# MLP ramp of a hybrid encoder: residual and first-phase tiles in one pool, casts of late right factors ordered behind PSUM copies

## The chip, the cores and the metric

One core of one Trainium2 chip. The metric is the device time of one execution in microseconds (us), as the median of several runs. All times below are of the kernel before.

## The reference

Two layers on a sequence of 1024 tokens with 1024 features, float32: layer 0 mixes tokens with grouped-query attention, layer 1 with a bidirectional gated linear attention. Behind each mixer stands a dense MLP with a squared ReLU and 4096 hidden features; a final RMSNorm ends it. The change touches only the two MLPs:

```
def sq_relu_mlp(h, w_in, w_out):
    return jnp.square(jax.nn.relu(h @ w_in)) @ w_out
...
        h = h + sq_relu_mlp(rmsnorm(h, norm_mlp[i]), mlp_w_in[i], mlp_w_out[i])
```

## The kernel before

Activations lie transposed: features on the 128 partitions, 512 tokens (one half) along the free dimension. Each float32 product is made of three matmuls on rounded parts: a value is split into a high part (a cast on ScalarE, L97) and a low part (a subtraction on VectorE, L98), and high by high, high by low and low by high are added in PSUM (`mm_into`, L463).

`layer_rest` (L755) runs twice, once per layer: the mixer's output projection with the residual, then the MLP's first phase (`h @ w_in`, `mlp_in`), then its second (`mlp_out`). Both phases use a scheme of seven products for two-by-two blocks in place of eight. P1 to P7 each multiply a combination of weight blocks (the left factor: `Weights.combine`, L483, four VectorE steps L487 to L490, then a split) with a combination of blocks of the normalised residual (the right factor). The right factors of the first phase are made once per layer:

- B11, B21: the normalised first half (features 0 to 511 and 512 to 1023); T1 and T2: differences, made at L831 and L841. These serve P1, P2, P5 and P6.
- T3: four subtractions at L846, then four splits; it serves P7.
- B22: four splits of the normalised second half, for P3.
- T4: four subtractions at L853, then four splits, for P4.

The first phase walks over eight groups of four hidden tiles each; a group's seven products have 24 matmuls each, twelve per output tile. P1, P6, P7 and P4 accumulate in two "a" banks of PSUM (there are four), P2 in two "b" banks, P5 and P3 in two "b" banks again (there are only two of these, so the P5 of the next group needs the P3 of this one drained). Results leave PSUM in `run` (L540): P1, P5 and P6 by a copy on ScalarE (L558) into a tile s1, s5 or s2; P2, P7 and P3 by an addition on VectorE (L561), followed by ReLU and square on ScalarE (L506, L507); P3 also by three subtractions (L570 to L575); P4 by L506, L507 and L582. The finished tiles are stored to DRAM by SyncE (L534).

The order of the first two groups (the ramp) is P1 and P2 of group 0, P1 and P2 of group 1, then P5, P6, P7, P3 of group 0, P5 and P6 of group 1, P4 of group 0, P7, P3 and P4 of group 1. The left factor of a step is prepared two steps ahead (`prep`), the weights' blocks are loaded by SyncE (L481) as soon as one of six buffers is free.

The framework that the kernel is written in orders the instructions of each engine when the program is built: by priority, which is the order of the source unless `tc.high_priority(offset=...)` shifts it, among what its plan takes to be ready. The queues are then worked off in that order. In the kernel before, T3, B22 and T4 carry negative offsets of 40, 80 and 160, so that they stand later than where they are written.

The sixteen residual tiles lie in a pool `hp`, next to scratch tiles (`tmpr`). The first phase's result tiles other than s1 of the first two groups come from a pool `hid` of sixteen that is opened behind T4, once `hp` and the scratch are closed, on the same memory:

```
859                     mid.close()
860                     hid_pool.append(pool_of(one, "hid", 16, side="right"))
861                     for g, p in ramp:
...
867                         run(g, p)
```

Of the kernel before, what the change touches and what calls it, by code (L numbers as in the profile page):

```python
# [23 lines left out]
F32 = mybir.dt.float32  # L24
F32R = mybir.dt.float32r
AF = mybir.ActivationFunctionType
# [5 lines left out]
P = 128  # L32
# [3 lines left out]
HN = S // 2  # L36
# [5 lines left out]
NCH = S // P  # L42
LEAD = 22
LAG = 3
LATER = 40


C_MIX0, C_MLP0, C_MIX1, C_MLP1, C_FIN, C_QA, C_QB, C_KA, C_KB, C_OUT, NCOL = 0, 8, 16, 24, 32, 40, 41, 42, 43, 44, 46
# [2 lines left out]
def trunk_kernel(tc, xT, wqk, wv, wo, win0, wout0, gqk, gv, gvz, gr, gate, gwo, win1, wout1, cols, rope, cmat, yT):  # L51
    nc = tc.nc

    def pool_of(stack, name, bufs=1, side=None):
        return stack.enter_context(tc.tile_pool(name=name, bufs=bufs, side=side, reuse_waits="tile"))

    with ExitStack() as top:
# [135 lines left out]
        with ExitStack() as at:  # L193
            env.raw, env.tmp = wraw, pool_of(at, "tmp")
            right = at.enter_context(ExitStack())
# [18 lines left out]
            x = (xh, xl)  # L214
# [224 lines left out]
            for step in range(256):  # L439
                h = step // 16  # L440
# [63 lines left out]

        def relu_sq(t, src):
            nc.scalar.activation(out=t, in_=src, func=AF.Relu)  # L506
            nc.scalar.activation(out=t, in_=t, func=AF.Square)  # L507

        B11, B21, B22, T1, T2, T3, T4 = range(7)
        RIGHT = {"P1": B11, "P2": B21, "P3": B22, "P4": T4, "P5": T1, "P6": T2, "P7": T3}  # L510
# [1 line left out]
        def mlp_in(win, x, hx, hid, hid_dram):  # L512

            blocks = win.rearrange("(j i a) p (b n) -> j a b p i n", i=2, a=2, b=2)
            ngr = NPAIR // 2
            weights, factors, alpha, beta, tiles = {}, {}, {}, {}, {}

            def begin(g):
                if g < ngr:
                    weights[g] = Weights(lambda r, c: blocks[g, r, c], env.raw, ("11", "12") if g == 1 else ("22", "11", "21", "12"))  # L520

            def prep(g, p):
                factors[g, p] = weights[g].factor(p)

            def combine():
                weights[0].combine(False)
                begin(1)

            def reload():
                weights[0].load("22")  # L530
                weights[1].load("22", "21")

            def store(g, i, what, t):
                nc.sync.dma_start(out=hid_dram[what, 2 * g + i], in_=t)  # L534

            def tile_of(g, nm):
                pl = hx if g < 2 and nm == "s1" else hid
                return pl.tile([P, HN], F32, tag="hx", name=nm)

            def run(g, p):  # L540
                wh, wl = factors.pop((g, p))
                xs = x[RIGHT[p]]
                if p == "P1":
                    alpha[g] = [bank("a") for _ in range(2)]
                if p in ("P2", "P5"):
                    beta[g] = [bank("b") for _ in range(2)]
                for i in range(2):
                    ps = (alpha if p in ("P1", "P6", "P7", "P4") else beta)[g][i]
                    parts = []
                    for k in range(4):  # L550
                        ks = slice(i * HN + k * P, i * HN + k * P + P)
                        parts.append((wh[:, ks], wl[:, ks], xs[0][k], xs[1][k]))
                    mm_into(ps, parts, p in ("P1", "P2", "P5"))
                    t = tiles.setdefault((g, i), {})
                    if p in ("P1", "P6", "P5"):
                        nm = {"P1": "s1", "P6": "s2", "P5": "s5"}[p]
                        t[nm] = tile_of(g, nm)
                        nc.scalar.copy(out=t[nm], in_=ps)  # L558
                    elif p in ("P2", "P7", "P3"):
                        c = t[{"P2": "s1", "P7": "s5", "P3": "s2"}[p]]  # L560
                        nc.vector.tensor_tensor(out=c, in0=ps, in1=c, op=ALU.add)  # L561
                        relu_sq(c, c)
                        if p == "P2":
                            store(g, i, B11, c)
                        elif p == "P7":
                            store(g, i, B22, c)
                        else:
                            h11, h22 = t["s1"], t["s5"]
                            t1 = tile_of(g, "t1")
                            nc.vector.tensor_tensor(out=t1, in0=c, in1=h11, op=ALU.subtract)  # L570
                            store(g, i, T1, t1)
                            t["t2"] = t2 = tile_of(g, "t2")
                            nc.vector.tensor_tensor(out=t2, in0=h22, in1=t1, op=ALU.subtract)
                            store(g, i, T2, t2)
                            nc.vector.tensor_tensor(out=c, in0=h22, in1=c, op=ALU.subtract)  # L575
                            store(g, i, T3, c)
                    else:
                        c = tile_of(g, "h21")
                        relu_sq(c, ps)
                        store(g, i, B21, c)  # L580
                        t4 = tile_of(g, "t4")
                        nc.vector.tensor_tensor(out=t4, in0=c, in1=t["t2"], op=ALU.subtract)  # L582
                        store(g, i, T4, t4)

            rest = ("P5", "P6", "P7", "P3", "P4")
            steps = [(g, p) for g in (0, 1) for p in ("P1", "P2")] + [(g, p) for g in (0, 1) for p in rest]
            steps = steps[:8] + [(1, "P5"), (1, "P6"), (0, "P4")] + steps[11:]
            steps += [(g, p) for g in range(2, ngr) for p in ("P1", "P2") + rest]
            return steps, begin, prep, run, combine, reload
# [165 lines left out]
        def layer_rest(w, src, o, gcol, win, wout, last, ahead, begun):  # L755


            hid_dram = dram.tile([7, NPAIR, P, HN], F32, name=f"hid_dram{last}")
            hm_dram = dram.tile([KT, P, S], F32, name=f"hm_dram{last}")
            with ExitStack() as ph:  # L760
                env.raw = Turns((wraw, 2), (pool_of(ph, "mraw", 4), 4))
                with ExitStack() as one:
                    hx = pool_of(one, "hx", 4, side="right")
                    mid = one.enter_context(ExitStack())
                    hp = pool_of(mid, "hp", side="right")
                    scratch = mid.enter_context(ExitStack())
                    env.tmp = pool_of(scratch, "tmpr", side="right")
                    big2 = pool_of(one, "big2", 8)
                    ht = halves(KT)
                    at_slot = [(0, 0)] + [(4 + k, 1) for k in range(3, -1, -1)] + [(k, 1) for k in range(3, -1, -1)]  # L770
                    at_slot += [(4 + k, 0) for k in range(3, -1, -1)] + [(k, 0) for k in range(3, 0, -1)]
                    for m, half in at_slot:
                        ht[m][half] = hp.tile([P, HN], F32, name=f"h{m}_{half}")
                    x = [([None] * 4, [None] * 4) for _ in range(7)]
                    r = [None, None]

# [11 lines left out]
                        return t  # L788

                    todo = []  # L790
                    hid_pool = []
                    steps, begin, prep, run, combine, reload = mlp_in(win, x, hx, SimpleNamespace(tile=lambda *a, **k: hid_pool[0].tile(*a, **k)), hid_dram)
                    weights_ahead = iter(steps)
                    for half in range(2):
                        sums = SumSquares(nc.vector if half else nc.gpsimd)
                        for m in range(KT):
# [9 lines left out]
                            ps = begun.pop(0) if begun else proj("b" if m % 4 == 0 else "a", wm, o, half)  # L806
                            h = ht[m][half]
# [3 lines left out]
                            for _ in range(2):  # L811
                                if todo:
                                    k = todo.pop(0)
# [27 lines left out]
                        nc.vector.tensor_tensor(out=t2, in0=normed(4 + k, 1), in1=ht[k][0], op=ALU.subtract)  # L841
                        xsplit(T2, k, t2, big)
                    prep(*next(weights_ahead))
                    with tc.high_priority(offset=-LATER):
                        for k in range(4):
                            nc.vector.tensor_tensor(out=ht[k][1], in0=ht[4 + k][1], in1=ht[k][1], op=ALU.subtract)  # L846
                            xsplit(T3, k, ht[k][1], big)
                    with tc.high_priority(offset=-2 * LATER):
                        for k in range(4):
                            xsplit(B22, k, ht[4 + k][1], big)  # L850
                    with tc.high_priority(offset=-4 * LATER):
                        for k in range(4):
                            nc.vector.tensor_tensor(out=ht[4 + k][0], in0=ht[4 + k][0], in1=t2s[k], op=ALU.subtract)  # L853
                    scratch.close()
                    big3 = pool_of(one, "big3", 4)
                    with tc.high_priority(offset=-4 * LATER):
                        for k in range(4):
                            xsplit(T4, k, ht[4 + k][0], big3)
                    mid.close()
                    hid_pool.append(pool_of(one, "hid", 16, side="right"))  # L860
                    for g, p in ramp:
                        nxt = next(weights_ahead, None)
                        if nxt:
                            prep(*nxt)
                        if p == "P5":
                            begin(g + 1) if g else None
                        run(g, p)
                env.tmp = pool_of(ph, "tmp2", side="right")
                raw2 = pool_of(ph, "raw2", 4)
                hst = pool_of(ph, "hst", 3)  # L870
# [2 lines left out]
                ht = halves(KT)  # L873
# [397 lines left out]
```

## Time and profile before

| what | value |
|---|---|
| median of 3 runs | 2391.19 us (2389.13 to 2392.6) |
| the profiled execution, its own time | 2392.76 us |
| its span, first to last instruction | 2390.8 us |
| mean granted TensorE clock, share of full speed | 0.987 |
| busy share of TensorE / VectorE / ScalarE / GpSimd | 96% / 75% / 56% / 14% |
| the two MLP ramps in the span | about 648 to 734 us and 1740 to 1826 us |

In the profile's rows PE is TensorE's matmuls, PEld its weight loads, DVE VectorE, ACT ScalarE, POOL GpSimd and SPq the queue of SyncE, which issues DMAs. L12 is line 12 of the kernel. In a timeline each row has the start and the duration in us, the engine, the line, the operation, the tile written and the tiles read, the shapes and the count; a number in square brackets is the time that the engine stood idle before it, with what it waited for. Consecutive instructions of one engine overlap at their ends, so the pitch from start to start is shorter than the duration.

### The profile page before, as it was taken

What the parts mean: (1) busy time and instruction counts of PE and PEld (TensorE: products, weight loads), DVE (VectorE), ACT (ScalarE), POOL (GpSimd) and SP (SyncE); (2) the same over time, 40 slices, a digit from 0 to 9 for tenths busy, and PEclk for the clock granted to TensorE, in tenths of its full rate; (3) what the DMA queues carried; (4) which work ended last, traced back from release to release, by engine and by line L of the source; (5) the groups of instructions that cost most, each with busy time, mean ns of one, the idle gap of its engine ahead of it and who ended that gap; (6) DMA issues with size and microseconds to landing.
All of it is one profiled execution on the core that took longest, in us unless ns stands there. A gap on an engine that the chain in (4) does not pass through costs nothing. (4 is left out here: it accounts for less than half of the span.)

```text
span 2390.8 us, 29877 instructions
## 1 busy us (share of the span) xinstructions
PE 2302.1 (96%) x10710; PEld 1899.9 (79%) x10710; DVE 1781.9 (75%) x2502; ACT 1346.5 (56%) x2386; POOL 335.8 (14%) x267
## 2 busy tenths in 40 slices
PE   8889999999979999999999999999979999999996
PEld 6677777777868888888888888898868888888885
DVE  8989999995786565888776767667686656797785
ACT  7448888884455555543344755655455555543343
POOL 2434444443000000000012000000100000000003
PEclk9989999999989999999999999999989999999998
DMA  5442111104435546954522121115625445965422
GB/s 177 129 141 62 43 38 45 36 14 147 144 119 168 175 161 222 309 187 151 175 91 85 47 73 53 54 71 189 216 71 192 160 165 176 320 211 185 150 89 71
DMA packets 157796, 317.50 MB, mean 133 GB/s; under 512 B 15048, under 2 KB 17872, under 8 KB 157520
## 3 DMA queue, kind: packets, MB, share of 16 engines
q1 hardware_dynamic: 157648, 315.60, 39.6%
q8 instruction: 84, 1.38, 0.2%
q14 instruction: 64, 0.52, 0.1%
HBM read 223.20 MB, written 92.27 MB: 132 GB/s over the span
## 5 line engine op out<-in xcount | busy, mean ns | idle before, releaser
L98 DVE TENSOR_TENSOR wl<-raw,wh 128x1024 fp32r<-128x1024 f32 x293 | 360.5, 1230 | 199.9 <-ACT wh L97 198.0
L97 ACT CAST wh<-raw 128x1024 fp32r<-128x1024 f32 x293 | 307.4, 1049 | 325.5 <-PE ps_a L467 134.3
L97 ACT CAST hh<-hst 128x512 fp32r<-128x512 f32 x224 | 134.8, 617 | 247.2 <-PE ps_a L468 112.5
L148 POOL TENSOR_TENSOR sq<-sq 128x512 f32<-128x512 f32 x35 | 54.5, 1557 | 1399.4 <-ACT sq L146 785.2
L401 POOL TENSOR_TENSOR pl<-p,ph 128x512 fp32r<-128x512 f32 x128 | 181.8, 1421 | 198.7 <-ACT p L398 129.7
L467 PE MATMUL ps_a<-xl,wh 128*128 128x512 f32 x512 | 201.2, 393 | 0.0
L466 PE MATMUL ps_a<-xh,wh 128*128 128x512 f32 x512 | 200.8, 392 | 0.0
L466 PE MATMUL ps_a<-hh,wh 128*128 128x512 f32 x512 | 199.4, 389 | 1.4 <-ACT h L506 1.4
L468 PE MATMUL ps_a<-xh,wl 128*128 128x512 f32 x512 | 200.1, 391 | 0.0
L98 DVE TENSOR_TENSOR hl<-hst,hh 128x512 fp32r<-128x512 f32 x224 | 153.1, 702 | 63.1 <-ACT hh L97 62.3
L467 PE MATMUL ps_a<-hl,wh 128*128 128x512 f32 x512 | 199.3, 389 | 0.6 <-DVE hl L98 0.6
L468 PE MATMUL ps_a<-hh,wl 128*128 128x512 f32 x512 | 199.2, 389 | 0.0
L278 DVE TENSOR_REDUCE mx<-ps_b 128x1 f32<-128x512 f32 x256 | 169.5, 683 | 12.6 <-PE ps_b L277 10.2
L466 PE MATMUL ps_b<-xh,wh 128*128 128x512 f32 x384 | 150.2, 391 | 26.9 <-ACT s L558 26.9
L397 ACT ACTIVATE ph<-ps_a 128x512 fp32r<-128x512 f32 x248 | 148.2, 598 | 29.7 <-PE ps_a L391 27.4
L398 ACT ACTIVATE p<-ps_a 128x512 f32<-128x512 f32 x256 | 152.2, 596 | 1.0 <-POOL pl L401 0.2
L467 PE MATMUL ps_b<-xl,wh 128*128 128x512 f32 x384 | 149.9, 390 | 0.0
L468 PE MATMUL ps_b<-xh,wl 128*128 128x512 f32 x384 | 149.4, 389 | 0.0
L506 ACT ACTIVATE s<-s 128x512 f32<-128x512 f32 x96 | 60.7, 632 | 111.1 <-DVE s L561 111.1
L277 PE MATMUL ps_b<-k,q 128*128 128x512 f32 x256 | 105.8, 415 | 9.4 <-DVE mx L278 9.4
L466 PEld LDWEIGHTS ps_a<-xh,wh 128*128 128x128 f32 x512 | 96.9, 189 | 21.2 <-ACT s L558 0.9
L466 PEld LDWEIGHTS ps_a<-hh,wh 128*128 128x128 f32 x512 | 96.1, 188 | 22.1 <-ACT h L506 2.3
(277 smaller groups left out, 5986.3 us busy)
## 6 DMA issues: line engine op xcount, KB each, us to landing
raw<-in_win_dram SPq DMA_DIRECT2D x80, 512.0 KB, 3.7
raw<-in_wout_dram SPq DMA_DIRECT2D x80, 512.0 KB, 3.6
hst<-hid_dramFalse SPq DMA_DIRECT2D x56, 512.0 KB, 3.8
hst<-hid_dramTrue SPq DMA_DIRECT2D x56, 512.0 KB, 3.5
q<-q_dram SPq DMA_DIRECT2D x96, 128.0 KB, 2.8
hid_dramFalse<-s SPq DMA_DIRECT2D x48, 256.0 KB, 2.8
hid_dramFalse<-t SPq DMA_DIRECT2D x48, 256.0 KB, 3.2
hid_dramTrue<-s SPq DMA_DIRECT2D x48, 256.0 KB, 2.0
```

Source lines behind the costliest of these rows:

```text
L97: nc.scalar.copy(out=hi, in_=src)
L98: (leng or nc.vector).tensor_tensor(out=lo, in0=src, in1=hi.bitcast(F32), op=ALU.subtract)
L148: self.eng.tensor_tensor(out=sq, in0=self.acc, in1=sq, op=ALU.add)
L277: nc.tensor.matmul(ps, q1[h][:, c * P : c * P + P], kst[h // 4][0][:, HALF[half]], start=True, stop=True)
L278: nc.vector.tensor_reduce(out=mx[h][:, half * 8 + c : half * 8 + c + 1], in_=ps, axis=AX.X, op=ALU.max, negate=True)
L397: nc.scalar.activation(out=phh, in_=ps, func=AF.Exp)
L398: nc.scalar.activation(out=p, in_=ps, func=AF.Exp)
L401: (nc.vector if c % 2 == 0 else nc.gpsimd).tensor_tensor(out=pll, in0=p, in1=phh.bitcast(F32), op=ALU.subtract)
L466: nc.tensor.matmul(ps, wh, xh, start=start and i == 0, stop=False, skip_group_check=not start)
L467: nc.tensor.matmul(ps, wh, xl, start=False, stop=False, skip_group_check=not start)
L468: nc.tensor.matmul(ps, wl, xh, start=False, stop=i == len(parts) - 1, skip_group_check=not start)
L506: nc.scalar.activation(out=t, in_=src, func=AF.Relu)
```

## The change

The pool `hid` is opened before the residual is made, and the sixteen residual tiles are taken from it with the tag of the result tiles, in the order rows 0 to 3 and 4 to 7 of the two halves as shown. A result tile therefore takes the place of one residual tile. The subtractions and splits of T3, B22 and T4 become functions that are called in the ramp, after group 0's P5, P6 and P7; `tc.issue_after(ins)` queues those of their instructions that run on the engine of `ins` (ScalarE: the casts) behind it. `ins` is the last ScalarE instruction of the step: the copy of the second tile for P5 and P6, the square of the second tile for P7. No wait for that instruction's end is added, and nothing is said about the order on other engines.

```diff
         def relu_sq(t, src):
             nc.scalar.activation(out=t, in_=src, func=AF.Relu)
-            nc.scalar.activation(out=t, in_=t, func=AF.Square)
+            return nc.scalar.activation(out=t, in_=t, func=AF.Square)
...
                         t[nm] = tile_of(g, nm)
-                        nc.scalar.copy(out=t[nm], in_=ps)
+                        end = nc.scalar.copy(out=t[nm], in_=ps)
...
-                        relu_sq(c, c)
+                        end = relu_sq(c, c)
...
+                return end
...
                     hx = pool_of(one, "hx", 4, side="right")
-                    mid = one.enter_context(ExitStack())
-                    hp = pool_of(mid, "hp", side="right")
-                    scratch = mid.enter_context(ExitStack())
+
+                    hid = pool_of(one, "hid", 16, side="right")
+                    scratch = one.enter_context(ExitStack())
...
-                    at_slot = [(0, 0)] + [(4 + k, 1) for k in range(3, -1, -1)] + [(k, 1) for k in range(3, -1, -1)]
-                    at_slot += [(4 + k, 0) for k in range(3, -1, -1)] + [(k, 0) for k in range(3, 0, -1)]
-                    for m, half in at_slot:
-                        ht[m][half] = hp.tile([P, HN], F32, name=f"h{m}_{half}")
+                    for m0, half in ((0, 0), (0, 1), (4, 1), (4, 0)):
+                        for m in range(m0, m0 + 4):
+                            ht[m][half] = hid.tile([P, HN], F32, tag="hx", name="h")
...
-                    with tc.high_priority(offset=-LATER):
+
+                    def t3():
                         for k in range(4):
                             nc.vector.tensor_tensor(out=ht[k][1], in0=ht[4 + k][1], in1=ht[k][1], op=ALU.subtract)
                             xsplit(T3, k, ht[k][1], big)
-                    with tc.high_priority(offset=-2 * LATER):
+
+                    def b22():
                         for k in range(4):
                             xsplit(B22, k, ht[4 + k][1], big)
-                    with tc.high_priority(offset=-4 * LATER):
+
+                    def t4():
                         for k in range(4):
                             nc.vector.tensor_tensor(out=ht[4 + k][0], in0=ht[4 + k][0], in1=t2s[k], op=ALU.subtract)
-                    scratch.close()
-                    big3 = pool_of(one, "big3", 4)
-                    with tc.high_priority(offset=-4 * LATER):
+                        scratch.close()
+                        big3 = pool_of(one, "big3", 4)
                         for k in range(4):
                             xsplit(T4, k, ht[4 + k][0], big3)
-                    mid.close()
-                    hid_pool.append(pool_of(one, "hid", 16, side="right"))
+
+
+                    behind = {(0, "P5"): t3, (0, "P6"): b22, (0, "P7"): t4}
                     for g, p in ramp:
                         nxt = next(weights_ahead, None)
                         if nxt:
                             prep(*nxt)
                         if p == "P5":
                             begin(g + 1) if g else None
-                        run(g, p)
+                        end = run(g, p)
+                        if (g, p) in behind:
+                            with tc.issue_after(end.ins):
+                                behind[g, p]()
```

## Rows read from the trace of the kernel before

**Rows 1.** The page's first part: busy us, share of the span, count of instructions
```profile
PE 2302.1 (96%) x10710; PEld 1899.9 (79%) x10710; DVE 1781.9 (75%) x2502; ACT 1346.5 (56%) x2386; POOL 335.8 (14%) x267
```

**Rows 2.** Waits of TensorE over the span: total us, times, longest us
```profile
PE ps_b L466 <- ACT s L558: 26.9, 2, 13.4
```

**Rows 3.** Timeline of TensorE in the two ramps
```profile
669.72 0.39 PE L466 MATMUL ps_b<-xh,wh 128*128 128x512 f32 x1
...
675.16 0.39 PE L466 MATMUL ps_a<-xh,wh 128*128 128x512 f32 x1
...
680.38 0.39 PE L468 MATMUL ps_a<-xh,wl 128*128 128x512 f32 x1
694.19 0.80 PE L466 MATMUL ps_b<-xh,wh 128*128 128x512 f32 x1 [13.43 <-ACT s L558]
694.79 0.63 PE L467 MATMUL ps_b<-xl,wh 128*128 128x512 f32 x1
695.21 0.75 PE L466 MATMUL ps_a<-xh,wh 128*128 128x512 f32 x1
...
698.27 0.39 PE L467 MATMUL ps_a<-xl,wh 128*128 128x512 f32 x1
...
1772.14 0.39 PE L468 MATMUL ps_a<-xh,wl 128*128 128x512 f32 x1
1785.96 0.80 PE L466 MATMUL ps_b<-xh,wh 128*128 128x512 f32 x1 [13.43 <-ACT s L558]
...
1790.49 0.40 PE L468 MATMUL ps_a<-xh,wl 128*128 128x512 f32 x1
```

**Rows 4.** Windows: stretch, us, busy us by engine, granted clock, DMA share, GB/s
```profile
660.00:680.60 20.60, 20.60 (x92) 16.87 (x90) 20.60 (x31) 13.50 (x21) 0.00 (x0) 1.00 0.46 143
680.60:694.20 13.60, 0.17 (x2) 0.01 (x1) 13.60 (x20) 6.61 (x12) 0.00 (x0) 0.64 0.17 55
694.20:698.30 4.10, 4.10 (x10) 3.00 (x11) 1.21 (x3) 1.40 (x3) 0.00 (x0) 0.51 0.00 0
698.30:720.00 21.70, 21.70 (x97) 17.95 (x96) 11.14 (x14) 11.27 (x16) 0.00 (x0) 1.00 0.51 170
```

**Rows 5.** Timeline of ScalarE, first ramp
```profile
691.23 2.42 ACT L97 CAST xh<-h 128x512 fp32r<-128x512 f32 x4 [5.65 <-DVE h L853]
693.56 1.07 ACT L558 COPY s<-ps_b 128x512 f32<-128x512 f32 x2
```

**Rows 6.** Timeline of VectorE, first ramp
```profile
674.13 0.69 DVE L841 TENSOR_TENSOR t<-h,h 128x512 f32<-128x512 f32 x1
674.74 1.22 DVE L98 TENSOR_TENSOR wl<-raw,wh 128x1024 fp32r<-128x1024 f32 x1
675.87 0.69 DVE L98 TENSOR_TENSOR xl<-t,xh 128x512 fp32r<-128x512 f32 x1
...
681.82 1.22 DVE L487 TENSOR_TENSOR raw<-raw 128x1024 f32<-128x1024 f32 x1
682.96 0.68 DVE L98 TENSOR_TENSOR xl<-h,xh 128x512 fp32r<-128x512 f32 x1
...
690.51 2.49 DVE L853 TENSOR_TENSOR h<-h,t 128x512 f32<-128x512 f32 x4
692.92 2.49 DVE L98 TENSOR_TENSOR xl<-h,xh 128x512 fp32r<-128x512 f32 x4
```

**Rows 7.** Queue of SyncE: loads of weights, first ramp; then their landing time
```profile
673.64 4.44 SPq L481 DMA_DIRECT2D raw<-in_win_dram  x3
...
raw<-in_win_dram SPq DMA_DIRECT2D x5, 512.0 KB, 3.7
```

**Rows 8.** Timeline of TensorE near the end, then a window as in rows 4
```profile
2350.48 0.80 PE L165 MATMUL ps_a<-sqh,ones 128*128 128x512 f32 x1 [2.51 <-ACT sqh L97]
...
2353.63 0.41 PE L467 MATMUL ps_c<-hl,wh 128*128 128x512 f32 x1
...
2351.00:2352.00 1.00, 1.00 (x4) 0.74 (x3) 0.15 (x1) 0.00 (x0) 0.00 (x0) 0.50 0.00 0
```

More of the change, by code (lines that the diff above doesn't have):

```diff
@@ L44 @@
 LAG = 3
-LATER = 40
 C_MIX0, C_MLP0, C_MIX1, C_MLP1, C_FIN, C_QA, C_QB, C_KA, C_KB, C_OUT, NCOL = 0, 8, 16, 24, 32, 40, 41, 42, 43, 44, 46
@@ L578, in run @@
                         c = tile_of(g, "h21")
-                        relu_sq(c, ps)
+                        end = relu_sq(c, ps)
                         store(g, i, B21, c)
@@ L790, in layer_rest @@
                     todo = []
-                    hid_pool = []
-                    steps, begin, prep, run, combine, reload = mlp_in(win, x, hx, SimpleNamespace(tile=lambda *a, **k: hid_pool[0].tile(*a, **k)), hid_dram)
+                    steps, begin, prep, run, combine, reload = mlp_in(win, x, hx, hid, hid_dram)
                     weights_ahead = iter(steps)
```

## The prediction

> **What bounds the kernel now.** The page's busy shares say TensorE: 96% busy, VectorE 75% [rows 1]. So I read next what TensorE waits for. Over the span its largest entry is the first matmul behind L558's copies: two waits, 26.9 us together [rows 2]. Two waits means one per MLP: the ramp, the first two groups of the first phase.
>
> The PE timeline shows where [rows 3]. One product of one group is 24 matmuls, 5.44 us (P5 starts at 669.72, P6 at 675.16). Group 0's P5 and P6 end the run: the last matmul starts at 680.38, so the next was due at 680.61; it starts at 694.19. That is 13.58 us idle, then nine starts take 4.08 us (to 698.27) that take 2.04 at the pitch of 0.227: 15.6 us lost. The second MLP repeats it: due 1772.37, started 1785.96, ten starts in 4.53 instead of 2.27: 15.85. Together **31.5 us**, 1.3% of the time, the most that this change can give.
>
> By windows, VectorE is busy for all 13.6 us of the wait and the granted clock is on average 0.64 in it, 0.51 in the 4.1 us behind it, 1.00 before and after [rows 4].
>
> The ACT timeline shows the cause [rows 5]: P5's banks are full by 675.4, but their copies run at 693.56, directly behind the four casts of T4. Not the copy is slow (0.5 us each); it stands behind the casts of T3, B22 and T4, since its target pool lies where the residual's tiles lie and opens only after their last use. These casts wait for VectorE's subtractions (5.65 us for L853). VectorE has no gap from 660 to 694.2 by the windows [rows 4], to 695.4 by its timeline [rows 6]. So the ramp is bound by VectorE's queue, with all of its work put ahead of two copies that need none of it.
>
> **What the change does, part by part.** Pitches from start to start: four subtractions 2.41 us, so 0.60 each (L853 to the lo parts behind it); a weight's lo part or a combine step 1.14 (674.74 to 675.87) [rows 6].
>
> *One pool.* The first four tiles taken for results are those that held the residual's rows 0 to 3, first half; their last reader is L841, the last one at 674.13 [rows 6]. P5's copies run from about 672.9 and 675.6, P6's from 678.5 and 681.1: none waits for a tile, nor P7 for P6's copy. Removed: the 13.58 us wait.
>
> *T3 behind P5's last copy.* VectorE reaches T3 at 676.47, with the weights' lo part for P3 now behind it. P5's copies are done at 676.2, or a weight cast (1.0 us) later; four subtractions and four lo parts, 4.8 us, so T3 is complete by 681.3, or by 682.4 with the last cast late and P3's 1.13 filling in. P7 starts at 680.61 and reads its fourth quarter 2.04 us later, the lo part at 682.9. Cost 0; at most 1.8 if P7 waited for all of T3.
>
> *B22 behind P6's last copy.* Casts from 681.6 to 683.7; P3's weight lo and four B22 lo parts by 684.8. P3 is due at 686.05. Cost 0; hidden by P7.
>
> *Group 1's weights.* Combine 4.55 and lo part 1.13: 690.5; its P5 is due at 691.5. SP: of its three loads from 673.64 the last waited for P3's weight lo and left at about 677.7 [rows 7]; that lo part now ends at up to 682.4, and the load lands 3.7 us later [rows 7], 686.1. If it is one that the combine reads, the combine starts 1.3 us late with other vector work ready: 0 to 0.7. The rest of SP's queue (stores of results, later loads) keeps its order; POOL does nothing here [rows 4].
>
> *T4 behind P7's last square.* This is the part that costs. Group 1's P5 needs the two "b" banks, so P3's drains (L561) must be done. In program order VectorE has ahead of them: P7's drains 1.2, T4's subtractions 2.4 and lo parts 2.4, the lo part for group 1's P6 1.13. From 690.5 that is 697.6, and the first drain ends at 698.3. Cross-check from the trace: vector work ended at 695.4 [rows 6] without P7's drains and that lo part; plus 2.3 gives 697.7. So the wait that goes at 680.6 comes back, smaller, at 691.5, again for VectorE. Its size hangs on the order in that queue, which the trace of before does not show, since there nothing competed. Bounds: 0 (drains go first) and 6.9 us (698.4 less 691.5). I take a value between: T4's casts can be ordered only once all four subtractions are, so at 694.1 no T4 lo part is ready and the lo part for P6 fills in (the combine steps at 682 to 689 are interleaved with other work in the same way [rows 6]); it ends at 695.2. P6 of group 1 uses other banks, and its matmuls that need no lo weights (four, 0.9 us) can run at once, as two of P3's ran ahead of P7 at 694.19 [rows 3]. So TensorE loses 695.3 - 691.5 - 0.9 = **2.9 us**, and P3's drains are done before P6 ends.
>
> *The clock.* Does a wait of some 3 us cost speed? A wait of 2.51 us near the end was followed by matmuls at half rate: seven starts from 2350.48 to 2353.63 took 3.15 us instead of 1.59, and the granted clock was 0.50 from 2351 to 2352 [rows 8]. Nearest row, so 1.5 us; bounds 0 and the 2.26 of the long wait. The Trainium skill, page "TensorE: Matmul & The Clock Gate", section "HAM oscillation", says that a warm-up is paid at each gap anew, not once: by that, two separate gaps per ramp (P7 and P5) would each cost up to 2.26; the sum below would then give 2374.6, inside the range. The rows give P7 no gap.
>
> *Sum.* Per MLP 15.7 removed, 2.9 + 1.5 given back: 11.3 gained, 22.6 in both. VectorE's and ScalarE's instructions are the same in number; later steps are bound by TensorE [rows 4] and all shift. The profiled execution is 2392.76 (span 2390.8, 1.96 around it), so 2370.2; it stands 1.57 above the median of 2391.19, so **2368.6**.
>
> **The rivals.**
> *B, the whole vector queue first.* T4's lo parts and P6's go ahead of P3's drains: 6.9 idle and 2.04 of clock. For it: VectorE works off its queue in order, and T4 is written ahead of P3. Against: the drain is ready from 689.1, and any gap in T4's chain lets it through. Gain 31.5 - 17.9 = 13.6: 2377.6.
> *C, no wait.* Drains slip in ahead of T4: 2359.7. For it: T4 is needed only by P4, at 702. Against: program order.
> *N, the copies still wait.* If the tiles did not come free until T4, or T4's casts stayed in front, nothing would change: 2391. Against: L841's last read at 674.13.
> *S, VectorE stands behind each group of casts.* The order that the change writes is ScalarE's alone. If VectorE's queue has the lo parts of T3, B22 and T4 each directly behind their casts' late start, it idles for a whole group of casts each time: four at 0.5 to 0.6 us, about 2.7 twice, 5.2 with T4's squares (four at 0.65) ahead: 10.6 us. P3's drain ends at 708.9, P5 loses 17.5 and two restarts 4: 21.5 against 15.7, so 2391 + 12 = 2403. It decides from about 7 us of such idling on. Against it: VectorE idled nowhere in 34 us though T3, B22 and T4 had the same casts [rows 4 to 6]. The Trainium skill's table at the head of the same page calls the queues of ScalarE and VectorE strict first in, first out, eight deep: that speaks for S and B, for nothing overtakes a lo part whose cast is late.
>
> **How the numbers follow.** Chances: forecast 0.43, B 0.27, C 0.17, N 0.07, S 0.06. About 0.2% (4.8 us) is what a measurement can tell from no change. Forecast, B and C are all faster by more: 0.87; N is the same, 0.07; S slower, 0.06. The range runs from C's 2359 to B's 2379 (its clock at 2.26) and leaves out N and S, 0.13.
>
> **What would show it.** In the profile of after: TensorE's 13.4 us waits for L558 gone; copies of P5 near 673 and 676, ahead of T3's casts; a wait at group 1's P5 or P6 for VectorE (L561 or a weight's lo part), 2 to 7 us, in both ramps, with half-rate matmuls behind it; matmuls of P6 ahead of P5's. No such wait means C. A wait before P7 for T3's lo part would prove my T3 step wrong; VectorE idle between 676 and 698 with ScalarE as releaser means S; copies still near 693 mean N.

## The result, and the profile after

The changed kernel takes 2364.06 us (median of four runs, 2362.75 to 2364.93) against 2391.68 (four runs, 2389.13 to 2392.60): a ratio of 0.9885 with a 95% interval of 0.9873 to 0.9898. It is faster by 27.6 us, where 22.6 was forecast; 2368.6 was predicted, in a range of 2359 to 2379. The profiled execution took 2364.93, its span is 2362.9 against 2390.8.

Most line numbers are lower by one: L97 of before is L96, L98 is L97, L466 to L468 are L465 to L467, L558 is L557, L561 is L560; T3's subtractions (L846) are L845, T4's (L853) are L854.

The page's busy times of the changed kernel, against [rows 1]:

```profile
PE 2299.3 (97%) x10710; PEld 1898.8 (80%) x10710; DVE 1780.8 (75%) x2502; ACT 1343.9 (57%) x2386; POOL 335.5 (14%) x267
```

All engines have the same number of instructions and nearly the same busy time. What went was waiting: TensorE idled for 2390.8 - 2302.1 = 88.7 us before and 2362.9 - 2299.3 = 63.6 now, 25.1 less. The waits of TensorE over the span of the changed kernel (total us, times, longest us) have no entry for L557's copies, which stood at 26.9 in [rows 2]. Two small entries came in its place:

```profile
PE ps_a L465 <- ACT xh L96: 2.5, 2, 1.2
PE ps_a L467 <- DVE wl L97: 1.8, 2, 0.9
```

The timeline of TensorE shows where these stand, in the first ramp, in the second, and then the place near the end that [rows 8] showed of before:

```profile
680.65 0.39 PE L465 MATMUL ps_a<-xh,wh 128*128 128x512 f32 x1
...
692.23 0.39 PE L466 MATMUL ps_a<-xl,wh 128*128 128x512 f32 x1
693.85 0.73 PE L465 MATMUL ps_a<-xh,wh 128*128 128x512 f32 x2 [1.23 <-ACT xh L96]
695.49 0.50 PE L467 MATMUL ps_a<-xh,wl 128*128 128x512 f32 x1 [0.90 <-DVE wl L97]
...
1769.83 0.40 PE L466 MATMUL ps_a<-xl,wh 128*128 128x512 f32 x1
1771.44 0.74 PE L465 MATMUL ps_a<-xh,wh 128*128 128x512 f32 x2 [1.22 <-ACT xh L96]
1773.09 0.50 PE L467 MATMUL ps_a<-xh,wl 128*128 128x512 f32 x1 [0.90 <-DVE wl L97]
1773.42 0.47 PE L465 MATMUL ps_a<-xh,wh 128*128 128x512 f32 x1
1773.68 0.63 PE L466 MATMUL ps_a<-xl,wh 128*128 128x512 f32 x1
...
1777.29 0.40 PE L465 MATMUL ps_a<-xh,wh 128*128 128x512 f32 x1
...
2324.03 0.50 PE L164 MATMUL ps_a<-sqh,ones 128*128 128x512 f32 x1 [2.51 <-ACT sqh L96]
2324.36 0.39 PE L467 MATMUL ps_c<-hh,wl 128*128 128x512 f32 x1
```

P7 starts at 680.65, right behind P6, where it waited until 694.19 [rows 3]. The run is unbroken until 692.23. The next matmul was then due at 692.46; the engine does two of P4 (0.45 us at the pitch of 0.227) and has all it needs again at 695.49. So each ramp now loses 695.49 - 692.46 - 0.45 = 2.58 us to waits. In the first ramp full speed follows at once. In the second, most matmuls up to 1777.29 run at half rate (0.63 us each): ten starts from 1773.42 take 3.87 us instead of 2.27, 1.6 us more. The windows, columns as in [rows 4], say the same of the clock:

```profile
680.60:694.20 13.60, 12.37 (x55) 9.88 (x54) 13.60 (x18) 9.36 (x15) 0.00 (x0) 1.00 0.31 97
694.20:698.30 4.10, 3.20 (x14) 2.32 (x13) 4.10 (x7) 1.16 (x3) 0.00 (x0) 1.00 0.54 175
1771.80:1778.00 6.20, 5.30 (x17) 3.88 (x16) 6.20 (x10) 3.02 (x7) 0.00 (x0) 0.72 0.36 124
```

TensorE is busy for 12.37 us of the 13.60 in which it did 0.17 before, and VectorE is still busy for all of both stretches: its work has not shrunk, it no longer holds TensorE. The timeline of ScalarE shows why, against [rows 5]:

```profile
672.69 0.59 ACT L557 COPY s<-ps_b 128x512 f32<-128x512 f32 x1
...
675.43 0.58 ACT L557 COPY s<-ps_b 128x512 f32<-128x512 f32 x1
...
677.25 1.22 ACT L96 CAST xh<-h 128x512 fp32r<-128x512 f32 x2 [0.29 <-DVE h L845]
678.37 0.58 ACT L557 COPY s<-ps_a 128x512 f32<-128x512 f32 x1
...
681.38 0.58 ACT L557 COPY s<-ps_a 128x512 f32<-128x512 f32 x1
681.86 2.18 ACT L96 CAST xh<-h 128x512 fp32r<-128x512 f32 x4
...
693.20 2.16 ACT L96 CAST xh<-h 128x512 fp32r<-128x512 f32 x4
```

P5's copies run at 672.69 and 675.43 instead of 693.56, P6's at 678.37 and 681.38; the casts of T3 begin behind P5's second copy, those of B22 (681.86) behind P6's, those of T4 are at 693.20. VectorE's timeline, against [rows 6], holds the cause of what is left:

```profile
676.52 1.89 DVE L845 TENSOR_TENSOR h<-h 128x512 f32<-128x512 f32 x3
...
690.67 1.22 DVE L489 TENSOR_TENSOR raw<-raw 128x1024 f32<-128x1024 f32 x1
691.80 2.49 DVE L854 TENSOR_TENSOR h<-h,t 128x512 f32<-128x512 f32 x4
694.21 1.22 DVE L97 TENSOR_TENSOR wl<-raw,wh 128x1024 fp32r<-128x1024 f32 x1
695.35 2.49 DVE L97 TENSOR_TENSOR xl<-h,xh 128x512 fp32r<-128x512 f32 x4
697.76 1.28 DVE L560 TENSOR_TENSOR s<-ps_b,s 128x512 f32<-128x512 f32 x2
```

T4's four subtractions (691.80) stand ahead of the lo part of the weights for group 1's P6 (694.21), and T4's four lo parts ahead of P3's two drains (697.76). P5 needs the drains, P6 the lo weights, and TensorE has run out of everything else. T4's casts, which the first of the two waits names, only let the two matmuls of P4 in between: what P6 goes on with at 695.49 is the lo part, which VectorE starts at 694.21, behind T4's last subtraction without a gap, and ends at 695.43.

**Where the 27.9 us of span came from.** Each landmark in TensorE's timeline is earlier by so much: the first matmul of the first MLP's second phase 12.85 us (968.34 before, 955.49 now; its first phase began 0.05 later), the first of the second layer's projections 13.40 (1280.01, 1266.61), the first of the second MLP's first phase 14.11 (1738.68, 1724.57), of its second phase 25.70 (2060.30, 2034.60), the matmul with the 2.51 us wait 26.45 (2350.48, 2324.03), the end 27.9. So 12.9 lie in the first MLP's first phase, 11.6 in the second's, and 1.45 behind the wait near the end: before, half-rate matmuls followed it [rows 8], here 2324.36 follows at full speed. The remaining 1.95 lie in between, 0.7 of it in the second layer's mixer.

### The profile page after: what moved, and what is told of

It reads as the page before. It is cut to its first block, busy times and chain, and to the rows that moved or that the text cites. A ratio compares the mean times of both kernels' runs of the same rounds, so it can differ in the third digit from the quotient of the medians.

```text
span 2362.9 us, 29859 instructions
## 1 busy us (share of the span) xinstructions
PE 2299.3 (97%) x10710; PEld 1898.8 (80%) x10710; DVE 1780.8 (75%) x2502; ACT 1343.9 (57%) x2386; POOL 335.5 (14%) x267
## 5 line engine op out<-in xcount | busy, mean ns | idle before, releaser
L97 DVE TENSOR_TENSOR wl<-raw,wh 128x1024 fp32r<-128x1024 f32 x293 | 360.7, 1231 | 202.3 <-ACT wh L96 200.7
L96 ACT CAST wh<-raw 128x1024 fp32r<-128x1024 f32 x293 | 307.4, 1049 | 331.3 <-PE ps_a L466 131.6
L96 ACT CAST hh<-hst 128x512 fp32r<-128x512 f32 x224 | 134.7, 617 | 244.4 <-PE ps_a L467 113.2
L465 PE MATMUL ps_a<-xh,wh 128*128 128x512 f32 x512 | 199.7, 391 | 2.5 <-ACT xh L96 2.5
L467 PE MATMUL ps_a<-xh,wl 128*128 128x512 f32 x512 | 199.7, 391 | 1.8 <-DVE wl L97 1.8
L466 PE MATMUL ps_a<-xl,wh 128*128 128x512 f32 x512 | 200.8, 392 | 0.0
L465 PE MATMUL ps_a<-hh,wh 128*128 128x512 f32 x512 | 199.3, 389 | 1.2 <-ACT h L505 1.2
L97 DVE TENSOR_TENSOR hl<-hst,hh 128x512 fp32r<-128x512 f32 x224 | 153.1, 703 | 62.6 <-ACT hh L96 61.8
L466 PE MATMUL ps_a<-hl,wh 128*128 128x512 f32 x512 | 199.3, 389 | 0.6 <-DVE hl L97 0.6
L467 PE MATMUL ps_a<-hh,wl 128*128 128x512 f32 x512 | 199.2, 389 | 0.0
L466 PE MATMUL ps_b<-xl,wh 128*128 128x512 f32 x384 | 149.4, 389 | 0.0
L467 PE MATMUL ps_b<-xh,wl 128*128 128x512 f32 x384 | 149.4, 389 | 0.0
L465 PE MATMUL ps_b<-xh,wh 128*128 128x512 f32 x384 | 149.4, 389 | 0.0
L467 PEld LDWEIGHTS ps_a<-xh,wl 128*128 128x128 f32 x512 | 96.7, 189 | 23.1 <-DVE wl L97 2.7
L465 PEld LDWEIGHTS ps_a<-xh,wh 128*128 128x128 f32 x512 | 96.2, 188 | 23.4 <-ACT xh L96 3.3
```

What stands on the lines that cost most here:

```text
L96: nc.scalar.copy(out=hi, in_=src)
L97: (leng or nc.vector).tensor_tensor(out=lo, in0=src, in1=hi.bitcast(F32), op=ALU.subtract)
L465: nc.tensor.matmul(ps, wh, xh, start=start and i == 0, stop=False, skip_group_check=not start)
L466: nc.tensor.matmul(ps, wh, xl, start=False, stop=False, skip_group_check=not start)
L467: nc.tensor.matmul(ps, wl, xh, start=False, stop=i == len(parts) - 1, skip_group_check=not start)
```

## The experiments

The theory: the shared pool frees the copies; that T3, B22 and T4 also stand late in VectorE's queue is needed to collect the gain; and the 2.58 us per ramp that are left are VectorE's order, with T4 ahead of the lo weights and of the drains that the two "b" banks wait for. The rivals: it is the ordering edge on ScalarE that gains, or that costs what is left; what is left comes from ScalarE's casts of T4, which the waits name as releaser; or there is nothing to be had beyond the copies. All runs were made in two groups, beside runs of the kernel before with medians of 2391.03 and 2392.04.

**Without the ordering edge** (`no_order`): the calls stay where they are.

```
-                            with tc.issue_after(end.ins):
+                            if True:
                                 behind[g, p]()
```

> The changed kernel with the ordering edge taken away: the casts of T3, B22 and T4 are called at the same places, nothing ties them to the PSUM copies. My theory: in the changed kernel's trace the casts already stand behind the copies because they are written behind them and their inputs come later, so the edge moves nothing: the same time as the changed kernel, 2364 within 2 us, no wait of 13 us at P5's copies. Rival (the edge is what lets the copies pass): the casts go ahead of the copies again and part of the 27 us is lost, 2375 to 2390. As the repeat of an unchanged order it would also show whether the half-rate matmuls of the second ramp (1773 to 1777 in the changed kernel's trace, none in the first) belong to the kernel or to the execution: to the execution, I expect.

Measured: 2368.33 (2362.98 to 2370.51), ratio 0.9901 (0.9886 to 0.9916), an interval that overlaps the changed kernel's. The median is 4.3 above the changed kernel's, and 2.3 above what was expected. The order of the instructions is the same on every engine as in the changed kernel, so the edge states only what the place of the calls in the source gives already, and the difference is put down to the execution. The timeline of TensorE in this kernel's two ramps, with one row from the end of the first MLP:

```profile
694.44 0.74 PE L465 MATMUL ps_a<-xh,wh 128*128 128x512 f32 x2 [1.23 <-ACT xh L96]
696.08 0.80 PE L467 MATMUL ps_a<-xh,wl 128*128 128x512 f32 x1 [0.89 <-DVE wl L97]
696.67 0.63 PE L465 MATMUL ps_a<-xh,wh 128*128 128x512 f32 x1
...
1265.85 0.63 PE L465 MATMUL ps_b<-hh,wh 128*128 128x512 f32 x1
...
1777.11 0.74 PE L465 MATMUL ps_a<-xh,wh 128*128 128x512 f32 x2 [1.23 <-ACT xh L96]
1778.74 0.50 PE L467 MATMUL ps_a<-xh,wl 128*128 128x512 f32 x1 [0.89 <-DVE wl L97]
```

The waits are those of the changed kernel within 0.01 us. But the half-rate matmuls (0.63) now stand in the first ramp and not in the second, and seven more run from 1265.85, behind waits of 1.01 and 0.73 us; the changed kernel has the same two waits there and no half-rate matmul behind them. Over both kernels, one order of instructions gave times from 2362.75 to 2370.51 in eight runs: a difference of a few us between the kernels below can lie within that.

**The pool alone, lateness by offsets** (`pool_only`): T3, B22 and T4 are written ahead of the ramp, as before, with the offsets of before.

```
-                    behind = {(0, "P5"): t3, (0, "P6"): b22, (0, "P7"): t4}
+                    for times, late in ((1, t3), (2, b22), (4, t4)):
+                        with tc.high_priority(offset=-40 * times):
+                            late()
+                    behind = {}
```

> One pool as in the changed kernel, but T3, B22 and T4 written ahead of the ramp with the negative offsets of 40, 80 and 160 of the kernel before, no edge. Theory (the pool is what held the copies): the wait of 13 us stays gone; in VectorE's queue B22's first lo part now stands behind combine steps, at about 688.2 instead of 682.5, so P3 of group 0 (due 686.1) starts about 2 us late and loses about 3 us in all, while the wait at group 1's P5 and P6 shrinks below 1 us: 2363 to 2368. Rival (the placing of the casts is half of the gain): 2375 or more.

Measured: 2363.34 (2362.28 to 2364.68), ratio 0.9884 (0.9868 to 0.9901). The pool with the old way of being late has the whole gain. Its waits stand elsewhere; the timeline of TensorE:

```profile
687.66 0.50 PE L466 MATMUL ps_b<-xl,wh 128*128 128x512 f32 x1 [1.65 <-DVE xl L97]
...
1764.91 0.50 PE L466 MATMUL ps_b<-xl,wh 128*128 128x512 f32 x1 [1.64 <-DVE xl L97]
```

P3 waits for B22's first lo part, which VectorE reaches behind a combine step and the lo weights. Two places for the same work in VectorE's queue, two different waits, about the same time.

**The pool alone, nothing late** (`pool_early`): as above, without offsets.

```
-                    behind = {(0, "P5"): t3, (0, "P6"): b22, (0, "P7"): t4}
+                    for late in (t3, b22, t4):
+                        late()
+                    behind = {}
```

> One pool as in the changed kernel, but T3, B22 and T4 written ahead of the ramp without any offset: the copies have their tiles, but VectorE's queue has all of the late factors' work first. Theory (the order of VectorE's queue sets what is left of the wait): P7's lo weights come at about 686 instead of 675.9, so TensorE loses about 4.6 us there, and about 2.5 at group 1's P5 and P6, with half-rate matmuls behind each, 0 to 2 us: 2372 to 2380. Rival (with the tiles free the place of the casts is worth nothing): 2363 to 2367.

Measured: 2372.26 (2370.33 to 2372.55), ratio 0.9919 (0.9903 to 0.9934), some 8 us slower than the changed kernel. The timelines of TensorE, then of VectorE:

```profile
686.01 0.50 PE L467 MATMUL ps_a<-xh,wl 128*128 128x512 f32 x1 [3.19 <-DVE wl L97]
...
687.08 0.63 PE L465 MATMUL ps_a<-xh,wh 128*128 128x512 f32 x1
...
1767.75 0.50 PE L467 MATMUL ps_a<-xh,wl 128*128 128x512 f32 x1 [3.18 <-DVE wl L97]
...
1769.01 0.62 PE L466 MATMUL ps_a<-xl,wh 128*128 128x512 f32 x1
```

```profile
682.93 1.89 DVE L854 TENSOR_TENSOR h<-h,t 128x512 f32<-128x512 f32 x3
684.74 1.22 DVE L97 TENSOR_TENSOR wl<-raw,wh 128x1024 fp32r<-128x1024 f32 x1
```

T4's subtractions now stand ahead of the lo weights for P7, and P7 waits for these, 3.2 us, with half-rate matmuls behind it in both ramps. The expectation had 4.6 us there and 2.5 more at group 1's P5 and P6; these wait for nothing in this trace. So of the 27.6 us the pool alone gives about 20 (2392.04 - 2372.26 = 19.8), and the late place of T3, B22 and T4 the rest, by this wait for VectorE.

**T4 behind P3** (`t4_behind_p3`):

```
-                    behind = {(0, "P5"): t3, (0, "P6"): b22, (0, "P7"): t4}
+                    behind = {(0, "P5"): t3, (0, "P6"): b22, (0, "P3"): t4}
```

> The changed kernel with T4 written behind P3 of group 0 instead of P7, banks unchanged. Theory (T4's subtractions stand ahead of the lo weights for P6 and of P3's drains in VectorE's queue): these now come at 691.8 to 694.1, so TensorE loses 0.5 to 1 us instead of 2.6 in each ramp, and T4 is still ready before P4 at 702: 2359 to 2362. Rival (the wait is for the banks or weights whatever stands in the queue): 2363.5 to 2365; a new wait at P4 for T4's lo parts would show that T4 is now late.

Measured: 2360.25 (2359.76 to 2361.34), ratio 0.9871 (0.9857 to 0.9886). The timelines of TensorE and then of VectorE:

```profile
691.36 0.50 PE L467 MATMUL ps_a<-xh,wl 128*128 128x512 f32 x1 [0.45 <-DVE wl L97]
...
1767.67 0.50 PE L467 MATMUL ps_a<-xh,wl 128*128 128x512 f32 x1 [0.26 <-DVE wl L97]
```

```profile
690.09 1.22 DVE L97 TENSOR_TENSOR wl<-raw,wh 128x1024 fp32r<-128x1024 f32 x1
691.22 1.29 DVE L560 TENSOR_TENSOR s<-ps_b,s 128x512 f32<-128x512 f32 x2
692.42 1.29 DVE L854 TENSOR_TENSOR h<-h,t 128x512 f32<-128x512 f32 x2
```

The lo weights and P3's drains now run ahead of T4's subtractions, and of the 2.58 us 0.45 and 0.26 are left. Only T4's place was changed, so T4's place was what cost them. Its casts on ScalarE moved with it; `t4_twice` below adds to VectorE's queue alone.

**Another pair of banks for group 1's P5** (`p5_c_banks`): T4 stays where the change put it.

```
-                    beta[g] = [bank("b") for _ in range(2)]
+                    beta[g] = [bank("c" if (g, p) == (1, "P5") else "b") for _ in range(2)]
```

> The changed kernel with group 1's P5 in the two c banks of PSUM, which nothing uses in the ramp, instead of the b banks that P3 of group 0 still holds. Theory: its weights' lo part is ready at 689.0, so P5 starts at 691.5 without a wait, P6's lo weights (695.3) and T4's lo parts (697.8) are ready before their products come (696.9 and 702.4). The 2.6 us of each ramp go, and half-rate matmuls with them: 2357 to 2359.5, and no wait of TensorE over 0.3 us between 680 and 720. Rival (VectorE's queue only delays the next product then): P6 or P4 of the ramp waits as long, 2363 to 2365.

Measured: 2361.21 (2359.43 to 2364.83), ratio 0.9877 (0.9862 to 0.9891); the median is 1.7 above the expected range. Windows over both ramps, columns as in [rows 4], then VectorE's timeline:

```profile
660.00:720.00 60.00, 60.00 (x267) 49.69 (x266) 54.26 (x74) 39.20 (x63) 0.00 (x0) 1.00 0.51 162
1740.00:1800.00 60.00, 60.00 (x267) 49.69 (x266) 55.30 (x76) 39.14 (x62) 0.00 (x0) 1.00 0.50 171
```

```profile
690.54 2.50 DVE L854 TENSOR_TENSOR h<-h,t 128x512 f32<-128x512 f32 x4
692.95 1.22 DVE L97 TENSOR_TENSOR wl<-raw,wh 128x1024 fp32r<-128x1024 f32 x1
```

TensorE is busy for every microsecond of both, at a granted clock of 1.00. P5 starts in the "c" banks without the drains, and while it runs for 5.44 us the lo weights for P6 and T4 get done. VectorE still has T4's subtractions ahead of the lo weights, so its order costs TensorE nothing as soon as there is a product to do meanwhile. This run does not part VectorE's share of the old wait from that of T4's casts, since P5 covers both. The Trainium skill's page "Perfetto Trace Analysis", section "Matmuls", tells independent groups of matmuls to rotate through different PSUM banks, so that emptying one lies beside the next; this run agrees, with both waits gone.

**Twice T4's subtractions** (`t4_twice`): four more, whose results nothing reads, ahead of T4's own.

```
                         for k in range(4):
+                            spare = env.tmp.tile([P, HN], F32, tag=("rs_t", "rs_r", "sqh", "sql")[k], name="spare")
+                            nc.vector.tensor_tensor(out=spare, in0=ht[4 + k][0], in1=t2s[k], op=ALU.subtract)
+                        for k in range(4):
```

> The changed kernel with T4's four subtractions done twice, the first time into tiles that nothing reads: 2.4 us more of VectorE ahead of P6's lo weights in each ramp, the order of every other instruction kept. Theory: TensorE's loss at group 1's P6 grows from 2.6 to 5.0 us in each ramp, and half-rate matmuls follow in both: 2369 to 2374. Rival (VectorE has slack there; the wait is for banks or loads): as the changed kernel, 2362 to 2367.

Measured: 2376.24 (2375.90 to 2380.32), ratio 0.9938 (0.9925 to 0.995): slower than the changed kernel by 12, and 2.2 above the expected range. The timeline of TensorE in the first ramp and behind it, then a window in the second ramp:

```profile
694.96 0.50 PE L465 MATMUL ps_a<-xh,wh 128*128 128x512 f32 x1 [2.96 <-ACT xh L96]
...
697.25 0.79 PE L467 MATMUL ps_a<-xh,wl 128*128 128x512 f32 x1 [1.79 <-DVE wl L97]
697.84 0.63 PE L465 MATMUL ps_a<-xh,wh 128*128 128x512 f32 x1
...
745.11 0.50 PE L465 MATMUL ps_b<-xh,wh 128*128 128x512 f32 x1 [1.01 <-DVE s L560]
```

```profile
1781.00:1785.50 4.50, 4.50 (x11) 3.35 (x12) 4.50 (x8) 1.63 (x3) 0.00 (x0) 0.50 0.38 117
```

The two waits grew from 1.23 + 0.90 to 2.96 + 1.79, by 2.62, for 2.41 us of VectorE's work: what is put in that queue comes out as TensorE's waiting, nearly one for one. That is 5.2 us of the 12 in two ramps. Half-rate matmuls are there in both ramps (the window's granted clock is 0.50, so 1.2 GHz of 2.4), and this profile has them behind the wait near the end too; at 745.11, behind the first ramp, TensorE waits 1.01 us more for a drain of VectorE (L560). Neither of these two was in the estimate.

**The same with the "c" banks** (`t4_twice_c_banks`), and **T4 behind P3 with the "c" banks** (`t4_p3_c_banks`): the edits above put together.

> The same doubled subtractions with group 1's P5 in the c banks. Theory: the 2.4 us more of VectorE lie beside P5's 5.4 us of matmuls; P6's lo weights come at 697.8 where its third matmul is due at 697.4, T4's lo parts at 700.2 ahead of 702.4: at most 0.5 us lost in each ramp, 2359 to 2363. Rival (the bank only hid a wait that moves on with VectorE's load): 4 us or more above the run with c banks alone, 2365 to 2368.

> Both: T4 written behind P3 and group 1's P5 in the c banks. Theory: each alone already leaves at most 0.5 us of wait in a ramp, so together they bring nothing more: 2359 to 2362. T4's lo parts now come at about 702, when P4 is due, so a wait of up to 0.5 us may stand there. Rival (what is left is the sum of two causes): 2356 to 2358.

Measured: 2361.90 (2359.54 to 2362.86), ratio 0.9873 (0.986 to 0.9887), and 2361.31 (2357.96 to 2362.27), ratio 0.987 (0.9856 to 0.9883). In both, TensorE is busy for 60.00 of 60 us around either ramp (660 to 720, 1740 to 1800). So the same extra work that cost 12 us costs nothing that can be told once P5 has banks of its own, and the two cures together are no better than one: with either, the ramp is at TensorE's pace within 0.5 us.

**Better than both kernels.** `t4_behind_p3` has the lowest median, 2360.25, and `p5_c_banks` 2361.21: some 3 to 4 us (0.15%) below the changed kernel. Their waits are gone, or nearly (0.45 and 0.26 us), as the traces show. The gain in time is at the edge of what can be told, since the changed kernel's own order of instructions scattered by more; but all four runs of `t4_behind_p3` (2359.76 to 2361.34) lie below all eight of that order.

## Why the prediction was right

**What bounds the kernel: right.** The 13.58 us wait was the copies' place behind T4's casts, for want of a tile. Taking the residual's and the results' tiles from one pool removed it in both ramps; 15.6 - 2.58 = 13.0 was to be gained in the first MLP by the rows, 12.9 was.

**One pool: right to 0.3 us.** Copies were foreseen at 672.9, 675.6, 678.5 and 681.1, and started at 672.69, 675.43, 678.37 and 681.38. P7 waits for nothing.

**T3 and B22: cost 0, as said.** VectorE reached T3 at 676.52 (foreseen 676.47), B22's casts run from 681.86 (681.6), and neither P7 nor P3 waits in the changed kernel. That the price was a matter of place is shown by `pool_only`, where P3 does wait for B22.

**Group 1's weights: right.** The third load left late, as foreseen (until 682.4). The queue of SyncE:

```profile
673.69 8.70 SPq L480 DMA_DIRECT2D raw<-in_win_dram  x3
```

VectorE stayed without a gap, and the combine's last step began at 690.67.

**T4 behind P7's last square: right in place, order and size.** The forecast was the lo part for P6 at 694.1 to 695.2 between T4's subtractions and its lo parts, and the first drain done at 698.3; the trace has 694.21, 695.35, and drains from 697.76. The four P6 matmuls with hi weights ran ahead, from 691.54. Predicted loss 2.9 us, measured 2.58. Not foreseen: two matmuls of P4 were ordered in between and split the wait, so that half of it is put down to T4's cast. The reason is the one given, VectorE's queue, as `t4_twice` and `t4_behind_p3` show.

**The clock: the term that was mis-sized.** 1.5 us was taken for each ramp from the one row of before. The trace has 0 in the first and 1.6 in the second, and `no_order`, in the same order of instructions, has them the other way round. So 3.0 was charged and 1.6 paid, and which ramp pays was not foreseeable from the rows. The rule weighed there, from the Trainium skill, page "TensorE: Matmul & The Clock Gate", section "HAM oscillation", is told of a loop that waits for a DMA at each step and pays at each anew. This case's waits of 2.58 us did not each pay: full speed followed in one ramp, half rate in the other.

**The sum: 5.3 too small a gain in the span.** 27.9 was gained where 22.6 was forecast. The first phases gave 12.9 and 11.6 instead of 11.3 each: 1.9 more, which the clock (1.4) and the wait (0.6) account for. 1.45 more lie behind the wait near the end, where before happened to have half-rate matmuls and after had none: no effect of the change, but of the execution from which the sum was made (4 of the 10 profiles here have them there). The last 1.95 lie in stretches that the change does not touch. So 3.4 of the 5.3 lie outside the first phases, and the terms of the mechanism itself were 1.9 off.

**The rivals.** B (all of T4 ahead, 6.9 us idle) had VectorE's order nearly right but left out that TensorE has P6 to do. C (no wait) did not come, but `p5_c_banks` has no wait: 2359.7 was worked out for C, its median is 2361.21. N and S fell: the copies moved, and VectorE has no gap between 676 and 698. The range's upper end is B with a clock loss of 2.26, which by the prediction's own terms is 2378 and not 2379.

## What to carry to other kernels

A pool that is opened on the memory of a closed one put its first user here behind the last reader of everything that lay there; where the tiles have the same shape, one pool lets each come free by itself. After such a wait is gone, look at the queue of the engine that was busy all along: put work with a late due time behind the drains that free PSUM, or give the next product other banks, and check with a run that doubles that work whether it is hidden. An explicit ordering edge is worth a look at the order that results: here it changed nothing.

## What the runs showed of the hardware that was not expected

Whether half-rate matmuls follow a short wait is not settled by the wait. Behind the split loss of 2.58 us they came in one ramp of two, the second with the changed kernel (1.6 us), the first with `no_order`. Behind the 2.5 us wait near the end they were there in 4 of the 10 profiles, the kernel before among them and the changed one not. Behind 1.01 and 0.73 us at the end of the first MLP they were there in `no_order` and not in the changed kernel, with the same order of instructions. Behind 1.65 us (`pool_only`) there were none; behind 3.19 (`pool_early`) and 2.96 + 1.79 (`t4_twice`) they came in both ramps. What tips it was not found. It may be the source of the several us by which runs of one kernel differ; the clock of each run speaks for it only in part: in `no_order` the mean granted clock is 0.991 in the two slowest runs (2369.65 and 2370.51) and 0.994 in the other two, but these are 4 us apart (2362.98 and 2367.01). Where the other runs lost it is not known, since only one execution of each was profiled.
